# Running the mLSTM steps beside the attention, and preparing the first attention head earlier, in a two-layer hybrid trunk on one Trainium2 core

## The chip, the core and the metric

The kernel runs on one core of one Trainium2 (trn2) chip, as one launch. The metric is device time in microseconds (us). A profiled execution gives a trace of every engine: PE (TensorE: matrix products and transposes), DVE (VectorE), ACT (ScalarE), POOL (GpSimd), and SP, which here only issues DMAs. PE's clock has two levels, 1.2 and 2.4 GHz; the profile's "granted clock" is the mean over a stretch, 1.00 where all of it ran at 2.4 GHz and 0.50 where all of it ran at 1.2 GHz.

## What is computed

Two layers (L0 and L1) on 512 latent and 256 context tokens of width 1024. Each layer makes one input projection, feeds its columns to three token mixers, joins their outputs to a 1024-wide y, applies an output projection, and then a gated feed-forward network. In layer 1 the context rows are read but not written.

```
za, zb, zm = split(modulate(rmsnorm(x)) @ w_in)
ya = rwkv7_mixer(za)     # scan over tokens, then "post": norm, bonus, gate
yb = mla_mixer(zb)       # q = up(norm(cq)), k,v = up(norm(ckv)); softmax(q k^T / sqrt(96)) v, 8 heads
ym = mlstm_mixer(zm)     # chunkwise, two directions, 4 heads
x  = x + gate1 * (concat(ya, yb, ym) @ w_out)
x  = x + gate2 * swiglu(modulate(rmsnorm(x)))
```

## The kernel before

Tokens stand in six tiles of 128 (four latent, two context); the transposed activations of width 1024 are 128-row pages. Matrix products that need full precision are done as three products of split operands (high part times high part, high times low, low times high).

The program is written as one sequence of operations, and a scheduler then places each engine's instructions, in an order in which it expects them to become ready. So code that is written later can be placed earlier if its inputs and buffers are there. What a buffer's pool allows (how many buffers a name has, and when the pool opens) limits this. Once placed, each engine's order is fixed.

The parts of a layer that matter here, in order:

- The **RWKV scan** and the rest of the input projection, ending at about 416 us in L0 and 1640 us in L1.
- **mLSTM** (`mlstm`, from L1182): a preparation (six tiles of transposes), then `chunk` for i = 0..5 and both directions, 12 steps in all. A step takes PSUM tiles `pbc`, `pbg`, `pss`, `pn`, each a bank of its own (pool `pb`, one buffer a name). `finish` (L1293) normalises two token tiles after steps 3, 4 and 5. The sums are kept in a page `hs` of the page pool.
- **Up-projection** (`mla_up`, L840): `heads` computes k for all heads (L954), then q for heads 0 to 3 and 4 to 7 (L959), normalises and rotates them, transposes them per head (`by_channel`, L904) and stores them to DRAM (`ktd`, `qtd`). Then V (L968). It is written behind the mLSTM, and the scheduler places the two together.
- **Attention** (`mla_attend`, L972). `load(h)` (L982) reads k and q of a head into a raw tile `kq` (two buffers) and splits each into a high and a low tile. `maxima` (L1000) takes each query block's row maximum over the keys (PE L1008 into one 1024-wide PSUM tile `mx`, DVE L1010), transposes it (L1014) and writes it as row 96 of q's high tile (ACT L1015), so that the score product subtracts it. `attend` (L1018) makes, for each of the six key tiles, the scores (PE L1028 to L1030, tile `st`, two buffers), the exponentials (ACT L1032) and the value product (PE L1034) into `po` (two buffers). Column 64 of V is one, which yields the sum: it is copied (ACT L1039), transposed (L1042), inverted (L1044), spread (L1047) and multiplied in (L1050). In L0 a second, smaller range handles the context queries. Head h+1 is loaded, and its maxima taken, while head h attends. The pools of `mla_attend` open when those of `mla_up` have closed, so head 0's load stands behind the up-projection.
- **RWKV post** (`rwkv_post`, L725): one call of its generator after each of the heads 0 to 6 (`POSTA`), the rest behind the last head.
- The loads of X for the residual (L1329, L1331) and the output projection (L262).

Of the kernel before, what the change touches and what calls it, by code (L numbers as in the profile page):

```python
# [26 lines left out]
POST = (0, 0, 0, 0, 0)  # L27
POSTA = (1, 1, 1, 1, 1, 1, 1, 0)
YS = 0
FI = 3  # L30
MP = ((0, .4), (-1, 0))
# [145 lines left out]
def trunk(ctx, tc, I, out, dbg=None):  # L177
# [547 lines left out]
    def rwkv_post(l, ctx_out, data, y, wk, psum):  # L725
# [34 lines left out]
        for n in range(nn):  # L760
# [8 lines left out]
            py, pgt = psum[0](), psum[0]()  # L769
            for i in range(2):  # L770
                pe.transpose(py[:, i * P:(i + 1) * P], yt[:, 2 * n + i], ident)
                pe.transpose(py[:, 256 + i * P:256 + (i + 1) * P], bt[:, i * P:(i + 1) * P], ident)
                pe.matmul(pgt[:, i * P:(i + 1) * P], g2[:, i * P:(i + 1) * P], gd[:, n * P:(n + 1) * P],
                          start=True, stop=True)
# [5 lines left out]
            ve.tensor_tensor(t, t, py[:, 256:512], ALU.add)  # L780
            ve.scalar_tensor_tensor(y[:, 0:2, n * P:(n + 1) * P], t[:, :].rearrange("p (j t) -> p j t", j=2), 0.5,
# [58 lines left out]
    def mla_up(l, ctx_out, lat, wk, pm, krt, post, marks):  # L840

        steps = iter(POST)

        def fill():
            for _ in range(next(steps, 0)):
                next(post, None)
# [6 lines left out]
        units = 0  # L853

        def up(act, wt, n, M):

            nonlocal units
            ps = pm.tile([P, 512], F32, name="up")[:, :M]
            i = int(MP[l][0] + units * MP[l][1])
            units += 1  # L860
            for k in range(len(act)):
              with behind(marks[i:i + 1] if i >= 0 else ()):
                mm3(ps, [x[:, n * P:(n + 1) * P] for x in act[k]], wt[k], k == 0, k == len(act) - 1)
# [35 lines left out]
        def by_channel(src, H, dst, n, h0):  # L899

            for a in range(0, H, 4):
# [3 lines left out]
                t = wk.tile([96, 4, P], F32, name="stg", bufs=3)  # L905
# [3 lines left out]
        def heads(act, r, wt, n0, n1, H, w, extra, dst, h0):  # L909
# [5 lines left out]
            for n in range(n0, n1):  # L915
# [3 lines left out]
                sq = wk.tile([P, 512], F32, name="ksq")[:, :H * w].rearrange("p (h b) -> p h b", b=w)  # L919
# [25 lines left out]
        sq = wk.tile([P, 512], F32, name="ksq")[:, :NT * 32].rearrange("p (n c) -> p n c", c=32)  # L945
# [6 lines left out]
        fill()  # L952
        for n in range(0, NT, 2):
            heads(ckv, rkv, wt, n, n + 2, 8, 64, (kr2[:, :, 0], ks), ktd, 0)  # L954
            fill()
        for a in range(2):
# [3 lines left out]
            fill()  # L960
# [9 lines left out]
        return V  # L970

    def mla_attend(l, ctx_out, y, V, wk, wk2, pm, pv, post):  # L972
        nq = T if ctx_out else TL
        psum = lambda: pm.tile([P, 512], F32, name="mx")
# [5 lines left out]
        ac.activation(idr, ident, AF.Copy)  # L980

        def load(h):  # L982

            r = []
            for src, i, n in ((ktd, 1, T), (qtd, 0, nq)):
                t = wk.tile([96, T], F32, name="kq", bufs=2)[:, :n]
                dma = sp.dma_start(out=t, in_=src[h, :, :n])
                hi, lo = (w.tile([97, T], F32R, name=f"k{i}{j}", bufs=2)[:, :n] for j, w in enumerate((wk, wk2)))
                if i == 0:
                    ac.activation(hi[0:96], t, AF.Copy, scale=gain)  # L990
                    ve.scalar_tensor_tensor(lo[0:96], t, gain, hi[0:96].bitcast(F32), ALU.mult, ALU.subtract)
                else:
                    ac.activation(hi[0:96], t, AF.Copy)
                    gp.tensor_tensor(lo[0:96], t, hi[0:96].bitcast(F32), ALU.subtract)
                    gp.memset(hi[96:97].bitcast(F32), 1.0)
                r += [hi, lo]
            loads.append(dma)
            return r

        def maxima(kq, q0, q1, k0):  # L1000
            kh, kl, qh, ql = kq
            w = q1 - q0
            mr = wk.tile([P, 4], F32R, name="mr")
            for n in range(q0, q1):
                ps = pm.tile([P, 1024], F32, name="mx", bufs=1)
                for a, b in ((0, 512), (512, T)):
                    if a >= k0:
                        pe.matmul(ps[:, a - k0:b - k0], qh[0:96, n * P:(n + 1) * P], kh[0:96, a:b],  # L1008
                                  start=True, stop=True)
                ve.tensor_reduce(mr[:, n - q0:n - q0 + 1], ps[:, :T - k0], AX.X, ALU.max)  # L1010
                yield
            pt = pm.tile([P, 512], F32, name="pt")
# [3 lines left out]
            yield  # L1016

        def attend(h, kq, q0, q1, k0):  # L1018
# [6 lines left out]
            for kt in kts:  # L1025
# [5 lines left out]
                e = wk2.tile([P, 512], F32, name="pe", bufs=EB)[:, :w]  # L1031
# [6 lines left out]
            row = wk2.tile([P, 512], F32, name="row")[o:o + 1, :w]  # L1038
            ac.activation(row, po[o:o + 1, :w], AF.Copy)  # L1039
            pd = pm.tile([P, 512], F32, name="pt")  # L1040
            for n in range(q1 - q0):
                pe.transpose(pd[:, n:n + 1], row[:, n * P:(n + 1) * P], one128[o:o + 1, 0:1])  # L1042
            r = wk.tile([P, 4], F32, name="rden")
            ve.reciprocal(r[:, :q1 - q0], pd[:, :q1 - q0])  # L1044
            bc = pm.tile([P, 512], F32, name="pt")
            for n in range(q1 - q0):
                pe.transpose(bc[:, n * P:(n + 1) * P], r[:, n:n + 1].to_broadcast([P, P]), ident)  # L1047
            yo = y[hr, 2 + h // 2, qs]
            i = ac.activation(yo, po[hr, :w], AF.Copy)
            done.append((i, ve.tensor_tensor(yo, yo, bc[hr, :w], ALU.mult)))  # L1050

        ranges = ((0, 4, 0), (4, 6, 512))[:2 if ctx_out else 1]
        loads, done = [], []
        kq = load(0)
        for _ in maxima(kq, *ranges[0]):
            pass
        for h in range(8):
            ahead = [maxima(kq, *g) for g in ranges[1:]]
            if h < 7:
                kq2 = load(h + 1)  # L1060
# [469 lines left out]
```

## Time and profile before

| | us |
|---|---|
| median of 3 runs | 2279.31 (2273.39 to 2284.45) |
| the profiled execution, its own time | 2283.55 |
| its span in the trace | 2281.8 |
| PE busy | 2159.2 (95%), mean granted clock 0.959 |
| DVE, ACT, POOL busy | 1381.9 (61%), 844.7 (37%), 314.2 (14%) |
| chain that ended last, by engine | PE 81%, DVE 10%, ACT 4%, DMA 2%, issue 2% |

Read it in two steps. First the whole: PE is near full everywhere on average, so a change can only save where PE stands still or runs at the lower clock. Then the stage: the busy share of a stretch, its granted clock, and the chain of waits through it tell who held PE up.

### The profile page before, as it was taken

How to read it: one execution, taken by the hardware profiler on the slowest of the kernel's cores; microseconds unless marked ns; L12 is line 12 of the kernel's file. 1: busy time of each engine (PE TensorE's matmuls, PEld its weight loads, DVE VectorE, ACT ScalarE, POOL GpSimd, SP SyncE). 2: the span in 40 equal slices, each digit the busy share in tenths (PEclk: the TensorE clock that was granted, in tenths of full speed). 3: DMA queues.
4: the chain of work that ended last, by engine and by line, in shares of the span. 5: the costliest groups of instructions: out<-in, count | busy, mean ns of one | idle time of the engine just before them, and what ended most of it. 6: DMA issues, size and time to landing. Idle time of an engine off the chain costs nothing.

```text
span 2281.8 us, 36365 instructions
## 1 busy us (share of the span) xinstructions
PE 2159.2 (95%) x14604; PEld 1780.9 (78%) x14604; DVE 1381.9 (61%) x2706; ACT 844.7 (37%) x1527; POOL 314.2 (14%) x482
## 2 busy tenths in 40 slices
PE   7999997997999999999999999999898998999999
PEld 4788886784668788888888878787685677888887
DVE  6687777895547766554444455788796545334343
ACT  4433333664552421122122354433473544222231
POOL 1022322332201100000000111113142211000000
PEclk9999997897999999999999989999697998999999
DMA  7241112232115334344432312211232122323323
GB/s 289 84 153 52 62 41 74 77 88 56 42 70 155 100 114 146 111 129 135 133 112 83 109 52 63 73 57 39 85 100 59 35 74 83 101 94 94 100 92 102
DMA packets 87352, 211.99 MB, mean 93 GB/s; under 512 B 10248, under 2 KB 33680, under 8 KB 86544
## 3 DMA queue, kind: packets, MB, share of 16 engines
q1 hardware_dynamic: 87184, 209.67, 29.2%
q8 instruction: 115, 1.88, 0.3%
q14 instruction: 53, 0.43, 0.1%
HBM read 187.62 MB, written 22.02 MB: 92 GB/s over the span
## 4 chain that ended last, share of the span: by engine, by line
PE 81%; DVE 10%; ACT 4%; DMA 2%; issue 2%; POOL 1%; SPq 0%; DVEq 0%; ACTq 0%; POOLq 0%
PE gm L262 57%; PE po L1034 4%; PE psm L585 2%; PE inv L660 2%; PE st L1028 1%; DVE cT L320 1%; PE st L1029 1%; PE st L1030 1%; PE mx L1008 1%; PE psm L514 1%; PE pB L700 1%; DVE wl L228 1%; PE psm L573 1%; ACT hu L365 1%; PE up L246 1%
## 5 line engine op out<-in xcount | busy, mean ns | idle before, releaser
L262 PE MATMUL gm<-hpage,wh 128*128 128x512 f32 (+1 forms) x3744 | 1001.7, 355 | 15.3 <-ACT hpage L227 8.9
L262 PEld LDWEIGHTS gm<-hpage,wh 128*128 128x128 f32 x3744 | 664.2, 191 | 119.8 <-ACT hpage L227 11.0
L262 PE MATMUL gm<-hpage,wl 128*128 128x512 f32 (+1 forms) x1872 | 657.4, 353 | 1.9 <-DVE wl L228 1.8
L227 ACT ACTIVATE wh<-wr 128x1024 fp32r<-128x1024 f32 (+2 forms) x214 | 221.6, 1036 | 560.7 <-PE gm L262 457.6
L262 PEld LDWEIGHTS gm<-hpage,wl 128*128 128x128 f32 x1872 | 358.1, 191 | 50.6 <-DVE wl L228 2.5
L228 DVE TENSOR_TENSOR wl<-wr,wh 128x1024 fp32r<-128x1024 f32 (+2 forms) x214 | 258.2, 1207 | 186.9 <-ACT wh L227 185.1
L262 PE MATMUL gm<-hid,wh 128*128 128x512 f32 (+1 forms) x1056 | 282.6, 356 | 0.0
L262 PEld LDWEIGHTS gm<-hid,wh 128*128 128x128 f32 x1056 | 185.6, 188 | 32.2
L262 PE MATMUL gm<-hid,wl 128*128 128x512 f32 (+1 forms) x528 | 187.4, 356 | 0.0
L1323 DVE SCALAR_TENSOR_TENSOR X<-gm,mod,X 128x512 f32<-128x512 f32 (+1 forms) x100 | 64.0, 643 | 191.0 <-PE gm L262 187.7
L320 DVE CUSTOM_DVE_ANT_0 cT<-wd,cB,mod_b 128x1024 f32<-128x1024 f32 x140 | 177.7, 1300 | 1.1 <-DMA wd<-in_mod_d 0.7
L1492 DVE SCALAR_TENSOR_TENSOR ft<-ft,gm 128x512 f32<-128x512 f32 x66 | 39.5, 598 | 153.0 <-PE gm L262 152.7
L1010 DVE TENSOR_REDUCE mr<-mx 128x1 fp32r<-128x768 f32 (+1 forms) x80 | 67.9, 848 | 83.8 <-PE mx L1008 83.6
L1034 PE MATMUL po<-pe,hpage 128*128 128x512 f32 (+1 forms) x224 | 112.2, 590 | 0.5 <-ACT pe L1032 0.4
L262 PEld LDWEIGHTS gm<-hid,wl 128*128 128x128 f32 x528 | 99.0, 188 | 16.1
L338 POOL TENSOR_TENSOR acc<-acc,sq 128x512 f32<-128x512 f32 (+1 forms) x15 | 23.9, 1601 | 604.0 <-ACT sq L337 604.0
L1032 ACT ACTIVATE pe<-st 128x512 f32<-128x512 f32 (+1 forms) x112 | 62.9, 563 | 89.8 <-PE st L1030 88.7
L227 ACT ACTIVATE hid<-ft 128x512 fp32r<-128x512 f32 x66 | 36.2, 549 | 128.4 <-DVE ft L1492 128.4
L1028 PE MATMUL st<-k,k 97*128 97x512 f32 (+1 forms) x112 | 78.0, 698 | 4.7 <-ACT k L1015 4.1
L1490 ACT ACTIVATE ft<-gm 128x512 f32<-128x512 f32 x66 | 33.9, 514 | 90.4 <-PE gm L262 90.3
L1008 PE MATMUL mx<-k,k 96*128 96x256 f32 (+1 forms) x144 | 46.3, 396 | 17.1 <-DVE mr L1010 9.9
L585 PE MATMUL psm<-pr,kb 64*128 64x128 f32 (+1 forms) x384 | 57.7, 308 | 1.4 <-POOL pr L555 1.4
(425 smaller groups left out, 3128.5 us busy)
## 6 DMA issues: line engine op xcount, KB each, us to landing
wr<-in_ffn_in SPq DMA_DIRECT2D x88, 512.0 KB, 3.5
wd<-in_mod_d SPq DMA_DIRECT2D x86, 512.0 KB, 3.8
wr<-in_w_in SPq DMA_DIRECT2D x44, 512.0 KB, 3.6
wr<-in_ffn_out SPq DMA_DIRECT2D x34, 448.0 KB, 3.4
wr<-in_w_out SPq DMA_DIRECT2D x20, 512.0 KB, 3.7
wr<-in_ffn_out SPq DMA_DIRECT2D x16, 512.0 KB, 3.6
zs<-ze SPq DMA_DIRECT2D x26, 256.0 KB, 2.0
X<-in_xT SPq DMA_DIRECT2D x16, 384.0 KB, 6.4
```

The costliest lines, as they stand in the source:

```text
L227: ac.activation(hi, src, AF.Copy)
L228: return en.tensor_tensor(lo, src, hi.bitcast(F32), ALU.subtract)
L262: pe.matmul(ps, x[:, j], act[k][y][:, a:b], start=(i == 0 and n == 0), stop=(i == len(kl) - 1 and n == 2))
L320: ve.tensor_tensor_reduce(out=t[:, s], in0=w, in1=cb[:, s], scale=1.0, scalar=modb[:, l, m:m + 1], op0=ALU.mult, op1=ALU.add, accum_out=mo ...
L585: pe.matmul(pa[j][:, p, c], flat(kb[hr, d, p, c]), flat(pr[hr, d, p, c, 0:nq]), start=True, stop=True)
L660: i = pe.matmul(v8(o)[hr, q], a[hr, d, p, c], b[hr, d, p, c], start=True, stop=True)
L1008: pe.matmul(ps[:, a - k0:b - k0], qh[0:96, n * P:(n + 1) * P], kh[0:96, a:b], start=True, stop=True)
L1010: ve.tensor_reduce(mr[:, n - q0:n - q0 + 1], ps[:, :T - k0], AX.X, ALU.max)
L1028: pe.matmul(ps, kh[0:97, ks], qh[0:97, qs], start=True, stop=False)
L1032: ac.activation(e, ps, AF.Exp, scale=QK_SCALE)
L1034: pe.matmul(po[:, :w], v, e, start=(kt == kts[0]), stop=(kt == kts[-1]))
L1323: return ve.scalar_tensor_tensor(X[:, m, a:b], ps, mods[l][:, 24 * which + 16 + m, s:s + 1], X[:, m, a:b], ALU.mult, ALU.add)
```

## The change

- The mLSTM becomes a generator. Its preparation runs first; then `mla_up` takes one step after every second call of `heads` (`SIDE[l][2]` = 2), and `mla_attend` takes the rest between key tiles, in proportion to the key tiles done. RWKV post is taken in the same way: two mLSTM steps, then one of post (`turns`). `POST`, `POSTA` and `MP` (which made some products wait for mLSTM marks) go.
- `between()`, behind the first half of the q projection, loads head 0 and takes its maxima. For this `mla_heads` has pools of its own (`q`, `px`).
- PSUM: all mLSTM and post tiles share the name `m` with two buffers (before, four names with a bank each). The maxima take two 512-wide tiles (two buffers) with one reduction each, and a maximum of the two. `po` and `pt` go from two buffers to one.
- `load` has no raw tile. k goes straight into a page of the page pool (the low half first holds the raw k). q goes into `qs`, one buffer in each of two pools, the low half holding the raw q. The gain is applied to q, the POOL subtraction to k, as before.
- After a head, one ACT copy of the whole of `po` to `ov` replaces the two copies L1039 and L1049, and y is written by the final multiplication.
- `hs` is kept in y itself instead of a page.

```diff
-POST = (0, 0, 0, 0, 0)
-POSTA = (1, 1, 1, 1, 1, 1, 1, 0)
+SIDE = (0, 60, 2), (0, 46, 2)
...
 # mla_up
         for n in range(0, NT, 2):
             heads(ckv, rkv, wt, n, n + 2, 8, 64, (kr2[:, :, 0], ks), ktd, 0)
-            fill()
+            step()
...
+            if a == 0:
+                between()
...
+        def load(h, wk):
+
+            k = hp.tile([P, 2, T], F32R, name="hpage")
+            q = wk.tile([97, 2, T], F32R, name="qs", bufs=1)
+            kh, kl, qh, ql = k[0:97, 0], k[0:97, 1], q[:, 0, :nq], q[:, 1, :nq]
+            raw = lambda t: t[0:96].bitcast(F32)
+            sp.dma_start(out=raw(kl), in_=ktd[h])
+            ac.activation(kh[0:96], raw(kl), AF.Copy)
+            gp.tensor_tensor(kl[0:96], raw(kl), raw(kh), ALU.subtract)
+            gp.memset(kh[96:97].bitcast(F32), 1.0)
+            loads.append(sp.dma_start(out=raw(ql), in_=qtd[h, :, :nq]))
+            ac.activation(qh[0:96], raw(ql), AF.Copy, scale=gain)
+            ve.scalar_tensor_tensor(ql[0:96], raw(ql), gain, raw(qh), ALU.mult, ALU.subtract)
...
 # maxima
-                ps = pm.tile([P, 1024], F32, name="mx", bufs=1)
...
-                ve.tensor_reduce(mr[:, n - q0:n - q0 + 1], ps[:, :T - k0], AX.X, ALU.max)
+                for i, (a, b) in enumerate(rng):
+                    ps = px.tile([P, 512], F32, name="mx")[:, :b - a]
+                    pe.matmul(ps, qh[0:96, n * P:(n + 1) * P], kh[0:96, a:b], start=True, stop=True)
+                    o = m2[:, i] if len(rng) == 2 else mr
+                    ve.tensor_reduce(o[:, n - q0:n - q0 + 1], ps, AX.X, ALU.max)
...
 # attend
-            po = pv.tile([P, 512], F32, name="po")
+            po = pv.tile([P, 512], F32, name="po", bufs=1)
...
-            ac.activation(row, po[o:o + 1, :w], AF.Copy)
+            ov = wk.tile([P, 512], F32, name="ov", bufs=2)[:, :w]
+            i = ac.activation(ov, po[:, :w], AF.Copy)
...
                 for _ in attend(h, kq, *g):
                     next(ahead, None)
                     next(ahead, None)
+                    at += 1
+                    while got < SN and (at - first) * (SN - got0) > (got - got0) * (over - first):
+                        next(side, None)
+                        got += 1
...
 # mlstm: chunk
-            pbc = pm.tile([P, 512], F32, name="pbc")
+            pbc = pm.tile([P, 512], F32, name="m")
...
-        hs = hp.tile([P, NT, 256], F32, name="hpage")
+        hs = [y[:, 6:8, n * P:(n + 1) * P] for n in range(NT)]
...
+        psb = lstack.enter_context(pool(f"pb{l}", 2, space=PSUM))
+        px = lstack.enter_context(pool(f"px{l}", 2, space=PSUM))
+        qp = lstack.enter_context(pool(f"q{l}", 1))
...
+            def between():
+                kq.append(heads[0](0, qp))
+                for _ in heads[1](kq[0], *RANGES[0], lambda: pm.tile([P, 512], F32, name="bc")):
+                    pass
```

How the placed order changes, at three places. (Line numbers are those of the program before or of the changed one, which are a few apart: maxima L1008 and L1005, scores L1028 and L1035, value products L1034 and L1041.)

PE in layer 0, the end of the up-projection, before (`up` and `bc` are the up-projection's tiles, `pss` mLSTM's, `mx` the maxima):

```order
L248 MATMUL up<-wh,hpage 128x512
L904 MATMUL bc<-c_id,kn 96x128 x8
L1307 MATMUL pss<-c_id,hpage 128x128 x6
L1008 MATMUL mx<-k_5829,k_5836 128x512
L1008 MATMUL mx<-k_5829,k_5836 128x256
```

PE in layer 0, head 0's maxima in the changed program (`m` is an mLSTM tile):

```order
L246 MATMUL up<-wh,hpage 128x384
L1271 MATMUL m<-mva,m_5616 128x65 x4
L1246 MATMUL m<-c_id,Q 128x128 x4
L1005 MATMUL mx<-hpage,qs 128x512
L1005 MATMUL mx<-hpage,qs 128x256
```

and the beginning of its attention, where the first scores follow the up-projection directly:

```order
L246 MATMUL up<-wh,hpage 128x512
L1237 MATMUL m<-c_id,sb 128x128
L901 MATMUL bc<-c_id,kn 96x128 x4
L1246 MATMUL m<-c_id,Q 128x128 x4
L901 MATMUL bc<-c_id,kn 96x128 x4
L1268 MATMUL m<-C_4685,qd 128x260
L1292 MATMUL m<-mva,kd_6137 128x260
L1237 MATMUL m<-c_id,sb 128x128
L1035 MATMUL st<-qs,hpage 128x512
```

The maxima moved from behind the last piece of the up-projection to a place some 67 rows ahead of the first scores, with the V projection between. Eight of the twelve mLSTM steps of layer 0 still stand ahead of the first scores; four, and two of three `finish`, now stand among the scores of heads 0 to 2.

ACT in layer 1, around the end of a head in the middle, before (`kq` the raw tile, `row` and `y` the copies of a finished head, `pt` the maxima's transpose):

```order
L1032 ACTIVATE pe<-st 128x512
L993 ACTIVATE k_17438<-kq 96x768
L1032 ACTIVATE pe<-st 128x512
L990 ACTIVATE k_17445<-kq,qkgain 96x512
L1039 ACTIVATE row<-po 1x512
L1015 ACTIVATE k_17334<-pt 1x512
L1049 ACTIVATE y<-po 64x512
L1032 ACTIVATE pe<-st 128x512 x4
```

and in the changed program:

```order
L1039 ACTIVATE pe<-st 128x512 x6
L225 ACTIVATE hpage<-y 128x512
L1014 ACTIVATE qs<-pt 1x512
L992 ACTIVATE qs<-qs,qkgain 96x512
L1046 ACTIVATE ov<-po 128x512
L1039 ACTIVATE pe<-st 128x512 x6
```

The conversion of the next-but-one head's q stood behind an exponential and converted an older raw tile; it now converts a tile that its own DMA fills, and the copy `ov` and the next head's exponentials stand behind it.

SP in layer 0, the last head loads and X, before:

```order
L987 DMA kq<-ktd 96x768
L987 DMA kq<-qtd 96x768
L1329 DMA X<-in_xT 128x768 x8
L318 DMA wd<-in_mod_d 128x1024 x4
```

and in the changed program:

```order
L991 DMA qs<-qtd 96x768
L987 DMA hpage<-ktd 96x768
L1335 DMA X<-in_xT 128x768 x8
L316 DMA wd<-in_mod_d 128x1024 x3
L991 DMA qs<-qtd 96x768 x3
L316 DMA wd<-in_mod_d 128x1024
```

X and three weight loads moved ahead of the q loads of heads 5, 6 and 7.

## Rows read from the trace of the kernel before

**Rows 1.** The page: busy time, share of the span, instructions of each engine
```profile
PE 2159.2 (95%) x14604; PEld 1780.9 (78%) x14604; DVE 1381.9 (61%) x2706; ACT 844.7 (37%) x1527; POOL 314.2 (14%) x482
```
**Rows 2.** Windows: stretch, length, busy PE, PEld, DVE, ACT, POOL, clock, DMA, GB/s
```profile
416.70:511.20 94.50, 88.36 (x543) 77.43 (x541) 89.27 (x304) 61.82 (x137) 35.91 (x54) 1.00 0.26 73
511.20:533.90 22.70, 6.24 (x18) 3.99 (x18) 11.58 (x23) 5.62 (x9) 3.98 (x3) 0.59 0.43 118
533.90:557.00 23.10, 21.71 (x80) 15.21 (x81) 9.90 (x20) 10.96 (x21) 2.55 (x2) 0.81 0.09 27
557.00:668.40 111.40, 105.74 (x489) 73.23 (x488) 57.62 (x113) 62.05 (x122) 22.49 (x17) 1.00 0.08 22
668.40:673.20 4.80, 3.78 (x28) 3.02 (x29) 1.46 (x5) 3.00 (x7) 0.00 (x0) 1.00 0.00 0
1650.00:1721.90 71.90, 68.59 (x433) 59.21 (x429) 63.26 (x206) 49.38 (x108) 28.44 (x44) 0.99 0.30 87
1721.90:1738.40 16.50, 9.81 (x33) 6.61 (x31) 11.46 (x42) 2.77 (x5) 4.00 (x4) 0.56 0.31 86
1738.40:1770.00 31.60, 29.60 (x85) 18.21 (x86) 16.56 (x33) 13.44 (x25) 6.62 (x6) 0.75 0.16 47
```
**Rows 3.** Chain that ended last, 511 to 535 us: start, us, what
```profile
514.04 6.21 DMA kq<-ktd
522.03 1.80 DVE k L991
523.85 3.23 DMA kq<-qtd
531.60 0.97 DVE mr L1010
```
**Rows 4.** The same chain, 1719 to 1740 us
```profile
1723.18 4.23 DMA kq<-ktd
1734.12 0.97 DVE mr L1010
```
**Rows 5.** The same chain, 664 to 690 us
```profile
672.36 0.35 SPq L1329
676.41 8.90 DMA wd<-in_mod_d
```
**Rows 6.** PE waits, 416 to 534 us: total, times, longest
```profile
PE pn L1263 <- DVE qd L1238: 2.9, 3, 1.5
PE pbc L1286 <- DVE qd L1238: 0.5, 1, 0.5
```
**Rows 7.** Tile kq, layer 1, its last line
```profile
DMA to landing us min/median/max: 3.0/3.1/4.2
```
**Rows 8.** ACT groups, 385 to 1860 us: count, busy, mean ns, idle before
```profile
L1032 ACT ACTIVATE pe<-st 128x512 f32<-128x512 f32 x96 | 56.9, 594 | 84.8 <-PE st L1030 83.8
L1258 ACT ACTIVATE m<-pbg,Q 128x128 f32<-128x128 f32 x80 | 22.8, 373 | 18.9 <-PE pn L1266 9.7 <-PE pbg L1241 9.1
L1039 ACT ACTIVATE row<-po 1x512 f32<-1x512 f32 x16 | 9.4, 588 | 12.1 <-PE po L1034 12.1
L990 ACT ACTIVATE k<-kq,qkgain 96x512 fp32r<-96x512 f32 x8 | 5.7, 710 | 0.0
L1039 ACT ACTIVATE row<-po 1x256 f32<-1x256 f32 x8 | 3.0, 375 | 1.3 <-PE po L1034 1.2
```
**Rows 9.** DVE groups, 385 to 1860 us
```profile
L1010 DVE TENSOR_REDUCE mr<-mx 128x1 fp32r<-128x768 f32 x64 | 61.1, 955 | 73.7 <-PE mx L1008 73.5
L1253 DVE TENSOR_TENSOR m<-pss,c_tri 128x512 f32<-128x512 f32 x10 | 6.8, 683 | 0.1
L1010 DVE TENSOR_REDUCE mr<-mx 128x1 fp32r<-128x256 f32 x16 | 6.8, 423 | 10.1 <-PE mx L1008 10.0
```
**Rows 10.** PE timeline, layer 1's last heads: start, us, operation, [idle before]
```profile
1827.93 0.41 PE L1042 MATMUL pt<-one,row 1*128 1x1 f32 x4 [0.22 <-ACT row L1039]
1828.64 0.47 PE L1028 MATMUL st<-k,k 97*128 97x512 f32 x1 [0.30 <-ACT k L1015]
1829.88 0.40 PE L1030 MATMUL st<-k,k 96*128 96x512 f32 x1
1830.12 0.51 PE L1008 MATMUL mx<-k,k 96*128 96x512 f32 x2
1830.47 0.60 PE L1047 MATMUL pt<-c_id,rden 128*128 128x128 f32 x4
1850.55 2.04 PE L1034 MATMUL po<-pe,hpage 128*128 128x512 f32 x4
```

More of the change, by code (lines that the diff above doesn't have):

```diff
@@ L780, in rwkv_post @@
             ve.tensor_tensor(t, t, py[:, 256:512], ALU.add)
+            pgt = psum()
+            for i in range(2):
+                pe.matmul(pgt[:, i * P:(i + 1) * P], g2[:, i * P:(i + 1) * P], gd[:, n * P:(n + 1) * P],
+                          start=True, stop=True)
             ve.scalar_tensor_tensor(y[:, 0:2, n * P:(n + 1) * P], t[:, :].rearrange("p (j t) -> p j t", j=2), 0.5,
@@ L838, in latent, with mla_up, step @@
         return parts, rs
[L840 to L846, printed above, removed]
+    def mla_up(l, ctx_out, lat, wk, pm, krt, between, side):
+        at = got = 0
+        def step():
+            nonlocal at, got
+            at += 1
+            if at % SIDE[l][2] == 0:
+                next(side, None)
+                got += 1
         nq = T if ctx_out else TL
@@ L980, in mla_attend @@
         ac.activation(idr, ident, AF.Copy)
[L982 to L998, printed above, removed]
@@ L1000, in maxima @@
-        def maxima(kq, q0, q1, k0):
+        loads = []
+        def load(h, wk):
[10 more added lines that the diff above has]
+            ve.scalar_tensor_tensor(ql[0:96], raw(ql), gain, raw(qh), ALU.mult, ALU.subtract)
+            return kh, kl, qh, ql
@@ L1016, in maxima, with mla_attend @@
             yield
+        return load, maxima, loads
+    RANGES = ((0, 4, 0), (4, 6, 512))
+    SN = 22
+    def mla_attend(l, ctx_out, y, V, heads, kq, qp, wk, pm, pv, side, got):
+        load, maxima, loads = heads
+        psum = lambda: pm.tile([P, 512], F32, name="pt")
         def attend(h, kq, q0, q1, k0):
@@ L1037, in attend @@
             o = 64 - 32 * (h % 2)
[L1038 to L1040 removed]
+            ov = wk.tile([P, 512], F32, name="ov", bufs=2)[:, :w]
+            i = ac.activation(ov, po[:, :w], AF.Copy)
+            pd = psum()
             for n in range(q1 - q0):
[L1042 removed]
+                pe.transpose(pd[:, n:n + 1], ov[o:o + 1, n * P:(n + 1) * P], one128[o:o + 1, 0:1])
             r = wk.tile([P, 4], F32, name="rden")
             ve.reciprocal(r[:, :q1 - q0], pd[:, :q1 - q0])
[L1045 removed]
+            bc = psum()
             for n in range(q1 - q0):
                 pe.transpose(bc[:, n * P:(n + 1) * P], r[:, n:n + 1].to_broadcast([P, P]), ident)
[L1048 to L1056, printed above, removed]
+            done.append((i, ve.tensor_tensor(y[hr, 2 + h // 2, qs], ov[hr], bc[hr, :w], ALU.mult)))
+        ranges = RANGES[:2 if ctx_out else 1]
+        done, at = [], 0
+        first, over, _ = SIDE[l]
+        got0 = got
         for h in range(8):
[L1058 removed]
+            ahead = [maxima(kq, *g, psum) for g in ranges[1:]]
             if h < 7:
[L1060 to L1061 removed]
+                kq2 = load(h + 1, (qp, wk)[(h + 1) % 2])
+                ahead.append(maxima(kq2, *ranges[0], psum))
             ahead = chain(*ahead)
@@ L1066, in mla_attend @@
                     next(ahead, None)
+                    at += 1
+                    while got < SN and (at - first) * (SN - got0) > (got - got0) * (over - first):
+                        next(side, None)
+                        got += 1
             for _ in ahead:
                 pass
-            with behind(done[-1]):
-                for _ in range(POSTA[h]):
-                    next(post, None)
             kq = kq2
-        for _ in post:
+        for _ in side:
             pass
@@ L1342, in behind, with turns @@
         return st
+    def turns(a, b):
+        while True:
+            n = 0
+            for g in (a, a, b):
+                for _ in g:
+                    n += 1
+                    yield
+                    break
+            if n == 0:
+                return
     early = ExitStack()
```

96 lines of the change are left out of this document (43 added, 53 removed).

## The prediction, made before the changed kernel was run

> **What bounds the kernel now.** The page comes first: PE is busy 95% of the span [rows 1], so time can only be won where PE stands or runs slowly. Next come the windows around the two places that the change touches [rows 2]. The reader is to see four things there. In the up-projection stages PE is busy 88.36 of 94.50 us (layer 0) and 68.59 of 71.90 (layer 1), at full clock. Then there is a hole in each layer: 22.70 us with PE busy for 6.24 at a granted clock of 0.59, and 16.50 us with 9.81 busy at 0.56. Behind each hole stands a stretch at reduced clock: 23.10 us at 0.81, and 31.60 us at 0.75. The rest of the attention of layer 0 is full again, 105.74 of 111.40. The chain of waits says who made the holes. In layer 0 it goes through the load of head 0's k (6.21 us to landing), a DVE subtraction, the load of its q (3.23), and then maxima, one block after the other [rows 3]; in layer 1 through the same load (4.23) and the maxima [rows 4]. So the holes are head 0's preparation, which nothing covers, and the slow stretches are what they leave behind: the clock is low in the hole, and full again only well into the attention.
>
> **The change, part by part.**
>
> *Head 0 moved into the projection.* The placed order shows it: the maxima now stand far ahead of the first scores, and the first scores come right behind the last pieces of the up-projection. What the holes hold of PE's work stays. Scaled to full clock it is at most 6.24 x 0.59 = 3.7 us and 9.81 x 0.56 = 5.5 us. Free: 22.7 - 3.7 = 19.0 and 16.5 - 5.5 = 11.0, together **30.0 us**. The two loads that are moved stand in SP's queue among the stores and weight loads of the projection; their landing (3 to 6 us [rows 3, 4]) has the V projection and the second half of q to hide under.
>
> *The slow stretches.* A stretch of length t at clock c would take t x c at full clock, if PE fills it. That frees 23.10 x 0.19 = 4.4 us and 31.60 x 0.25 = 7.9 us [rows 2], 12.3 in all. I take **10**, since a new short wait may bring a bit of it back; bounds 0 (if another hole appears) and 12.3.
>
> *mLSTM and post steps moved into the attention.* PE's own work only changes its place: it leaves a stage that PE fills to 94% and goes into one filled to 95% [rows 2], so I cost the move itself at nothing. What covers DVE's part is slack there: DVE is busy 57.62 of 111.40 us in the attention against 89.27 of 94.50 in the projection. If the attention had no PE work to hide under, the moved DVE work would show. Since the projection's DVE is relieved, its 6.1 and 3.3 us of PE idle might go too: 0 to 9.4 us, and I take 0, because other work (post's first part) is drawn into the same stage.
>
> *The end of layer 0's attention.* The last post block stood behind the last head: 4.80 us with PE busy 3.78 [rows 2]. Its work moves, its idle time goes: **1 us**.
>
> *Two reductions for one.* A 768-wide reduction costs 0.955 us. Instead: one of 256 (0.423) and one of 512, for which the nearest row is another 512-wide read of PSUM, 0.683 [rows 9]. That is 0.15 us more for each of 64 blocks, 10 us of DVE over both layers, plus a tiny maximum. In the attention DVE has 54 us to spare in layer 0 alone, so: nothing. Head 0's part, in the busy projection stage, is paid for by the steps that left.
>
> *One buffer for `po` and `pt`.* At the end of a head (or range) the next value product must wait for the copy `ov`. It is one ACT copy, 0.588 us at 512 columns and 0.375 at 256 [rows 8]; there are 16 of the first and 8 of the second. Before that product stand the six score products of the next head, from 1828.64 to 1830.12, 1.5 us [rows 10], which need no `po`. So I cost it at nothing. The upper bound is every copy in full: 16 x 0.588 + 8 x 0.375 = 12.4 us. The Trainium skill (Perfetto Trace Analysis, Optimizing Tensor Performance) says that independent matmul groups should rotate through different PSUM banks so that the evacuation of one overlaps the matmuls of the next, which the single `po` gives up; by that rule the sum would be about 12 us worse, 2260. No row before shows it, since `po` had two.
>
> *Two banks instead of four for mLSTM.* Each step's tiles now wait for each other. In the projection of layer 0 PE waited 3.4 us for mLSTM results with four banks [rows 6]. I take the same once more over both layers, **4 us**. The lower bound is 0; the upper is one further wait of four activations (4 x 0.373 = 1.5 us [rows 8]) for each of the 20 steps with an output, 30 us.
>
> *q without a raw tile.* The largest unknown. q of head h+2 goes into the buffer that head h reads until its last score, so its DMA starts there. Call that moment T. It lands at T + 3.1 [rows 7] and is converted by T + 3.8 (0.71 [rows 8]). Behind the conversion, on ACT, stand `ov` (T + 4.4) and the first exponential (T + 5.0). PE has, behind T, two value products (2.04 us), six scores (1.5) and a pair of maxima (0.35) [rows 10]: 3.9 us. Then it waits 0.5 for `ov`, and after the sum's transposes (0.25) another 0.35 for the exponential: 0.85 us, where 0.52 is waited at this place today (0.22 and 0.30 [rows 10]). I take 0.5 us for heads 2 to 7 of both layers, **6 us**. Bounds: 0, and the whole 3.8, 46 us. The loads of X and three weights now precede the q of heads 5 to 7 in layer 0's queue. Today the first weight lands at 685.3, 13 us after the first X load is issued [rows 5]; X can go once post is done, in head 3, so it should be over before head 5's q is due. I add nothing.
>
> **The sum.** 30.0 + 10 + 1 - 4 - 6 = 31 us. The profiled execution took 2283.55, so 2252.5; it lies 4.2 above the median of the runs shown, 2279.31, and on that footing the forecast is **2248 us**. Between holes closed with no new wait at all (30.0 + 12.3 + 1 + 9.4 = 52.7) and the rivals below lies all that I expect.
>
> **Rivals.**
>
> *Everything closes.* The new waits are hidden, and the projection loses its idle time: 2279.3 - 52.7 = 2227. For it: every new wait found has a cover of nearly its size. Against: the attention keeps 5% idle even with its second buffers [rows 2].
>
> *The banks give it back.* Every `ov` is exposed (12.4) and a third of mLSTM's bound (10): 2248 + 22 = 2270. For it: mLSTM steps stand between scores on PE, in an order fixed beforehand, so a late tile stops the scores behind it. Against: only four steps of layer 0 stand there.
>
> *The hole moves to head 1.* The change then does not do what it says: head 1's q cannot be loaded before the projection's buffers are released and its last store is out, so PE would stand at head 1's maxima instead. Price: load and conversion (4.2 + 0.7 [rows 4, 8]), twice, and the slow stretch behind (12.3): 22 us, 2270. Against: the order puts four key tiles of scores, over 6 us of PE work, ahead of those maxima.
>
> *Slower: q holds ACT at every head.* The conversion stands ahead of the next head's exponentials. If it comes as late as 3.8 us beyond PE's own work, scores fill their two buffers and PE stops; after such a stop part of the next stretch runs at half clock, as behind the holes. With 2 us lost that way (4.4 and 7.9 were lost behind the far longer holes): 12 x (3.8 + 2.0) = 70 us instead of 6, 2248 + 64 = 2312. The change breaks even at (31 + 6) / 12 = 3.1 us a head, and is slower by over 0.5% from 4.0. Against: the 3.9 us of PE work behind T. The Trainium skill (TensorE: Matmul & The Clock Gate, Architectural detail) calls ACT's queue strict FIFO, so that no exponential could pass the waiting conversion; the rows here show no wait long enough to test it.
>
> **How the numbers follow.** Chances: forecast 0.56 (2237 to 2260), everything closes 0.14, banks 0.17, hole moves 0.05, slower 0.08. The range leaves out the slower case and the tails of the two at 2270: **2226 to 2272**. A measurement of this kernel can tell about 0.5%, 11.4 us, from no change. Below 2267.9 lie the first two and almost half of the banks' case: 0.78. Within 0.5%: the rest of it and the moved hole, 0.14. Slower: 0.08.
>
> **What will show it.** If right, in the changed profile no stretch of 10 us between the projection and the attention has PE under 80% busy, and the granted clock there stays near 1.00 in both layers. Waits of scores, value products and sums on ACT stay under 1 us a head. DVE's share in the attention rises above 60%. It is wrong if a wait of PE on the q conversion, or on `ov`, repeats at each head with more than 2 us, if the time per head in layer 0 grows after its mLSTM steps are done, or if a hole stands at head 1.

## The result, and the profile after

| | before | changed |
|---|---|---|
| median, us | 2281.88 (4 runs, 2273.39 to 2290.82) | 2308.84 (4 runs, 2306.99 to 2311.31) |
| ratio | | 1.0118, 95% interval 1.0077 to 1.016 |
| span of the profiled execution, us | 2281.8 | 2305.9 |
| mean granted clock | 0.959 | 0.962 |

The change made the kernel slower by 1.2%; 1.4% faster had been forecast. The first row of the changed kernel's page answers to [rows 1]: PE is busy 11.6 us longer, and idle for 135.1 us instead of 122.6.

```profile
PE 2170.8 (94%) x14604; PEld 1783.4 (77%) x14604; DVE 1388.2 (60%) x2786; ACT 832.2 (36%) x1503; POOL 312.4 (14%) x482
```

The windows answer to [rows 2]. The columns are the same; the stretches are, in each layer, from the first to the last piece of the up-projection, from there to the first scores, and then two parts of the attention. Between the same events, the first two stretches of each layer before were:

```profile
422.10:509.90 87.80, 81.87 (x500) 72.29 (x500) 83.05 (x290) 57.79 (x127) 32.73 (x49) 1.00 0.28 79
509.90:533.90 24.00, 7.33 (x28) 4.84 (x26) 12.56 (x27) 6.88 (x10) 4.35 (x3) 0.62 0.41 112
1654.80:1718.90 64.10, 61.31 (x365) 53.40 (x364) 58.06 (x190) 45.19 (x98) 26.24 (x39) 1.00 0.33 95
1718.90:1738.40 19.50, 12.29 (x51) 8.79 (x49) 14.19 (x51) 5.60 (x11) 5.02 (x6) 0.62 0.26 73
```

and in the changed kernel:

```profile
421.80:523.30 101.50, 86.14 (x467) 70.48 (x466) 84.28 (x280) 55.48 (x116) 37.96 (x48) 0.95 0.29 77
523.30:527.90 4.60, 2.63 (x20) 1.84 (x17) 2.18 (x5) 4.56 (x10) 1.72 (x5) 1.00 0.77 191
527.90:551.00 23.10, 19.60 (x94) 13.88 (x94) 18.31 (x44) 12.69 (x26) 7.66 (x8) 1.00 0.22 67
551.00:683.10 132.10, 125.15 (x557) 88.39 (x558) 62.73 (x152) 63.88 (x124) 13.18 (x14) 0.92 0.16 54
1663.90:1739.10 75.20, 64.25 (x327) 51.60 (x325) 62.61 (x199) 42.32 (x86) 29.73 (x40) 0.93 0.33 89
1739.10:1752.10 13.00, 10.11 (x61) 8.47 (x60) 10.68 (x28) 7.45 (x14) 7.98 (x8) 0.87 0.34 99
1752.10:1783.70 31.60, 27.34 (x106) 18.84 (x105) 18.22 (x49) 14.99 (x31) 7.05 (x8) 0.84 0.18 51
1783.70:1876.50 92.80, 87.86 (x340) 56.63 (x338) 42.91 (x98) 40.65 (x71) 6.97 (x7) 0.94 0.12 40
```

In layer 0 the hole is closed: 4.60 us where 24.0 lay between the last piece and the first scores. But the projection, which PE filled to 93%, is now filled to 85% (86.14 of 101.50), and its last piece ends at 523.3 instead of 509.9. So the first scores of layer 0 start only 6 us earlier (527.90 against 533.86), and the attention then takes 155 us instead of 134. Part of that is work that moved there (PE is busy for 144.8 us instead of 127.5), part the clock (0.93 over the whole of it instead of 0.97). The time did not vanish with the hole; it moved to both sides of it.

In layer 1 the hole is not closed: 13.0 us remain of 19.5, better filled. Three of the four pairs of head 0's maxima still stand behind the last piece, which ends at 1739.1 (PE's timeline):

```profile
1736.15 0.62 PE L1005 MATMUL mx<-hpage,qs 96*128 96x512 f32 x2 [1.07 <-ACT qs L992]
1740.35 0.59 PE L1005 MATMUL mx<-hpage,qs 96*128 96x512 f32 x2
1742.09 0.71 PE L1005 MATMUL mx<-hpage,qs 96*128 96x512 f32 x2 [0.71 <-DVE m L1007]
1744.55 0.72 PE L1005 MATMUL mx<-hpage,qs 96*128 96x512 f32 x2
```

The projection there is 11 us longer as well (75.2 against 64.1).

Who holds PE inside the projection? Three of the largest waits of PE there (layer 0, 421 to 528 us: total, times, longest), all on other engines' results:

```profile
PE mx L1005 <- DVE m L1007: 5.1, 2, 3.1
PE bc L901 <- DVE kn L933: 4.4, 3, 3.3
PE m L1292 <- ACT m L1263: 1.8, 2, 1.4
```

The first is head 0's own maxima. The chain of waits through the second (start, us, what) shows a new guest: `yt` L761 is the end of RWKV post's first part (its statistics and norm), which the old program held behind head 0 and which now stands on DVE in front of the k norm (`kn` L933). The same wait of PE stands in e9 below (4.5 us), which leaves post free, and in neither e1 nor e4, which hold it.

```profile
435.84 2.02 DVE yt L761 x2
437.86 1.03 DVE kn L933
439.02 1.93 PE bc L901 x8
```

### The profile page after: what moved, and what is told of

Its sections match the earlier page's. It is cut to its first block, busy times and chain, and to the rows that moved or that the text cites. A ratio compares the mean times of both kernels' runs of the same rounds, so it can differ in the third digit from the quotient of the medians.

```text
span 2305.9 us, 36379 instructions
## 1 busy us (share of the span) xinstructions
PE 2170.8 (94%) x14604; PEld 1783.4 (77%) x14604; DVE 1388.2 (60%) x2786; ACT 832.2 (36%) x1503; POOL 312.4 (14%) x482
## 4 chain that ended last, share of the span: by engine, by line
PE 81%; DVE 9%; ACT 4%; DMA 3%; issue 1%; POOL 0%; SPq 0%; ACTq 0%; DVEq 0%; POOLq 0%
PE gm L260 58%; PE po L1041 4%; PE psm L583 2%; PE inv L658 2%; PE st L1035 1%; PE st L1036 1%; PE st L1037 1%; PE psm L512 1%; DMA qs<-qtd 1%; DMA lz<-zs 1%; PE pB L698 1%; PE mx L1005 1%; DVE hu L362 1%; PE psm L571 1%; DVE wl L226 1%
## 5 line engine op out<-in xcount | busy, mean ns | idle before, releaser
L1041 PE MATMUL po<-pe,hpage 128*128 128x512 f32 (+1 forms) x224 | 112.2, 594 | 1.1 <-ACT pe L1039 0.8
L1007 DVE TENSOR_REDUCE m<-mx 128x1 f32<-128x512 f32 (+1 forms) x128 | 66.0, 551 | 56.7 <-PE mx L1005 56.3
L1039 ACT ACTIVATE pe<-st 128x512 f32<-128x512 f32 (+1 forms) x112 | 62.3, 565 | 100.5 <-PE st L1037 99.7
L1035 PE MATMUL st<-qs,hpage 97*128 97x512 f32 (+1 forms) x112 | 76.7, 685 | 2.0 <-ACT stg L903 1.5
L1005 PE MATMUL mx<-hpage,qs 96*128 96x256 f32 (+1 forms) x144 | 50.7, 424 | 11.9 <-DVE m L1007 8.4
```

The costliest lines, as they stand in the source:

```text
L1005: pe.matmul(ps, qh[0:96, n * P:(n + 1) * P], kh[0:96, a:b], start=True, stop=True)
L1007: ve.tensor_reduce(o[:, n - q0:n - q0 + 1], ps, AX.X, ALU.max)
L1035: pe.matmul(ps, kh[0:97, ks], qh[0:97, qs], start=True, stop=False)
L1039: ac.activation(e, ps, AF.Exp, scale=QK_SCALE)
L1041: pe.matmul(po[:, :w], v, e, start=(kt == kts[0]), stop=(kt == kts[-1]))
```

## The experiments

All are given as the median and the ratio to the kernel before on the same chip. **First round**: undo one suspect each, then all three. e1 takes a step of post only when a head is done, and behind it:

```diff
 # turns(side, post)
+                if g is b and not done:
+                    continue
+                with behind(done[-1] if g is b else ()):
```

> Post of the RWKV mixer is taken only once head 0 has finished, as in the kernel before. Theory 'DVE in the projection': the 12 us a layer of post's statistics on DVE, which now stand inside the up-projection, hold up the k and q norms there; taking them out removes most of the extra idle time of that stage (19 us in layer 0 against 6 before, 21 us in layer 1 against 3): 2285 to 2298 us. Rival 'two banks': the up-projection lost time because mLSTM's tiles share two banks; then this run stays within 4 us of 2309 and PE still waits there on mLSTM tiles.

Measured: **2277.72**, 0.9982 (0.9967 to 0.9996): 31 us less than the change, more than its theory had. The windows of e1 (first piece to first scores but for the last 0.8 us; attention) show the projection 5 us shorter than the change's 101.5, with no hole behind it, and an attention as long as the change's 155.2. The projection also starts 4 us earlier. In the change part of the statistics stands in the end of the scan, but that this is the reason isn't shown: with post held, e11's projection starts at 425.4. In layer 1 the projection takes 62.6 us instead of 75.2.

```profile
417.30:513.40 96.10, 86.16 (x471) 72.24 (x470) 80.98 (x256) 54.19 (x111) 37.59 (x47) 0.93 0.30 83
514.20:669.00 154.80, 144.34 (x660) 102.70 (x661) 93.53 (x243) 82.30 (x164) 24.99 (x26) 0.94 0.18 60
```

e2 moves X:

```diff
-            with behind(loads[3:4]):
+            with behind(loads[7:8]):
                 xload(X, l)
```

> Only the loads of X wait, behind the q load of head 7 instead of head 3. Theory 'X in front of q': q of head 5 landed 8 us after its issue at 612 us because 3 MB of X and 1.5 MB of weights were ahead of it, its maxima came bunched behind head 4, and that head's slot took 22.7 us instead of 16.5; without X ahead of it the run gets 4 to 7 us faster, 2302 to 2305. Rival: the maxima of head 5 were late because of q's single buffer and would have been late anyway; then within 2 us of 2309.

Measured: **2299.69**, 1.0076 (1.0049 to 1.0103), 9 us less, again more than its theory had. SP's timeline of the change (start, us, operation) shows what e2 took away, and the loads of q tell it too (landing, minimum/median/maximum: 2.8/3.5/8.2 in the change, 2.8/3.1/3.9 in e2):

```profile
603.44 4.30 SPq L1335 DMA_DIRECT2D X<-in_xT  x8
607.78 2.83 SPq L316 DMA_DIRECT2D wd<-in_mod_d  x3
612.12 15.42 SPq L991 DMA_DIRECT2D qs<-qtd  x2
```

e3 gives q a third buffer:

```diff
-                kq2 = load(h + 1, (qp, wk)[(h + 1) % 2])
+                kq2 = load(h + 1, *((wk, 2) if (h + 1) % 3 else (qp,)))
```

> q has three buffers instead of two, so the load of head h+2 no longer waits for head h's last score. Theory 'q load exposed': PE's waits at the first maxima on the q conversion (1.25 us at head 4 of layer 0, 0.8 in layer 1) and the half-clock stretches behind them (some 2 us each) go: 6 to 14 us, 2295 to 2303. Rival: the end of each head is held by the single banks of po and pt, whatever q does; then within 3 us of 2309.

Measured: **2288.66**, 1.0022 (1.0005 to 1.0039), 20 us less, more than either case had. e4 has all three edits:

> All three edits together. If the three causes are separate and together hold most of what the closed holes won, the gains add: 2309 minus 20 to 35, that is 2274 to 2289, about the kernel before. If the two-bank rival holds, it stays above 2295.

Measured: **2268.97**, 0.994 (0.9919 to 0.9961), below its range. 40 us, not the sum of 60: the causes overlap.

**Second round**, on e4: what are the change's own parts worth? e5 puts head 0's preparation back behind the projection (`i` is the copy of its last piece):

```diff
-            if a == 0:
-                between()
...
+        with behind((i,)):
+            between()
         return V, got
```

> The kernel with all three edits (2269), but head 0's load and maxima stand behind the last piece of the up-projection, as before the change; everything else stays. Theory 'the hole was worth what the prediction said': 30 us of idle time and some 10 of low clock come back, less a few us that head 0's maxima cost inside the projection: 2294 to 2309. Rival: mLSTM steps, which may now stand in the hole, cover much of it; then 2272 to 2285.

Measured: **2264.77**, 0.9915 (0.9885 to 0.9944): head 0 late again, and no slower; it lies below both ranges. The windows of layer 0 of e4 (projection, attention) and then of e5 (projection, place of the hole, attention) show why:

```profile
420.20:518.70 98.50, 86.38 (x471) 72.58 (x470) 80.95 (x257) 54.01 (x111) 38.38 (x47) 0.93 0.29 81
519.50:664.80 145.30, 138.09 (x660) 97.80 (x661) 89.27 (x243) 81.24 (x164) 26.12 (x26) 0.99 0.20 64
```
```profile
419.40:499.00 79.60, 72.35 (x422) 62.03 (x421) 69.49 (x227) 49.70 (x102) 34.95 (x43) 1.00 0.35 98
499.00:517.00 18.00, 13.01 (x57) 8.65 (x54) 16.27 (x35) 9.15 (x15) 9.23 (x8) 0.77 0.39 117
517.00:658.60 141.60, 138.24 (x659) 98.99 (x658) 86.24 (x240) 77.45 (x159) 21.97 (x23) 0.97 0.16 53
```

First piece to first scores takes 99.3 us with head 0 early and 97.6 with it late. The projection alone is 19 us longer with it early, and PE's idle time on the whole way is the same: 12.1 us in e4's projection, 7.3 and 5.0 in e5's two stretches. In the place of the hole DVE is now busy 16.27 of 18.00 us, and PE 13.01 (in the kernel before, between the same two events, 12.56 and 7.33 of 24.0): mLSTM steps stand in it, which in the old program's layer 0 were all ahead of it. This pair tests layer 0 only: in layer 1, e4's first scores come 18.3 us behind the last piece and e5's 16.4, since there head 0's maxima stand behind the last piece in e4 too (three of four pairs, as in the change).

e6 and e7 move one bank from the maxima (two tiles to one) to mLSTM's tiles, and to `pt`:

```diff
-        px = lstack.enter_context(pool(f"px{l}", 2, space=PSUM))
+        px = lstack.enter_context(pool(f"px{l}", 1, space=PSUM))
```

> All three edits, and mLSTM's tiles get three banks; the maxima give one up and have one. Theory 'two banks': the waits of PE in front of mLSTM products in the projection (some 10 us in layer 0, 5 in layer 1 in the run with all three edits) are in good part turns of the two banks: 2258 to 2266. Rival 'DVE in the projection': those products wait for DVE's work whatever the banks, and the single tile of the maxima costs some: 2268 to 2280.

> All three edits, and the small tile at a head's end (transposed maxima, sums, reciprocals) gets a second bank; the maxima give one up. Theory 'single pt': the waits of 0.3 to 1.5 us at the ends of heads are its turns: 3 to 8 us, 2261 to 2266. Rival: the single tile of the maxima costs as much or more: 2268 to 2280.

Measured: **2362.97** (1.0345, 1.0317 to 1.0373) and **2339.19** (1.0245, 1.0221 to 1.027). They say nothing of the banks that were given, since the bank taken away cost 94 and 70 us against e4. The waits of PE in e6 (layer 0, 400 to 690 us) are led by

```profile
PE mx L1005 <- DVE m L1007: 15.0, 17, 2.5
```

(in e4 the same line has 0.6, once).

e8 holds all mLSTM steps that are written into the attention behind its first exponential.

> All three edits, and the mLSTM steps that are written into the attention may not be placed ahead of its first exponential: four stay in each projection, eight go into the attention. Theory 'DVE in the projection is the bound': moving their DVE work out shortens the projection by 10 us or more a layer, and the attention, with DVE under 60% busy, takes the PE work at its price: 4 to 12 us faster, 2257 to 2265. Rival 'moved work brings its waits': in the attention's order each step's chain PE, DVE, ACT, PE holds the scores behind it, and the time stays or grows: 2268 to 2285.

Measured: **2289.78**, 1.0037 (1.0016 to 1.0059): about 21 us slower than e4, the rival's way and beyond its range. Projection and attention of its layer 0:

```profile
420.30:510.40 90.10, 76.47 (x402) 64.16 (x400) 63.62 (x201) 47.38 (x89) 32.95 (x38) 0.91 0.31 87
511.20:673.00 161.80, 152.90 (x726) 109.49 (x727) 108.82 (x297) 87.98 (x186) 29.17 (x35) 0.95 0.18 58
```

The projection loses 8 us against e4 and the attention gains 16.5: here moved work was not free.

**Third round.** e9 is the change with only e5's edit, e10 the kernel before with only post's first part set free (`behind` dropped for head 0). e11 is e5 with four banks for mLSTM during the projection (the maxima's two open behind it), and e12 is e11 with head 0's loads free to go early.

> The change as it is (2309), with one thing undone: head 0's load and maxima stand behind the last piece of the up-projection again. Theory 'the hole was DVE's, not PE's': head 0's maxima cost the DVE-bound projection what they save behind it, so the time stays: 2300 to 2312. Rival, the prediction's step: holes and cold stretches are worth 30 to 40 us, so this run is slower than the change: 2335 to 2350.

> The kernel before, with one thing of the change: the first part of RWKV post (its statistics) is no longer held behind head 0 and may be placed as early as its inputs allow. Theory 'post's 12 us of DVE in the projection': 10 to 30 us slower than before, 2292 to 2312. Rival 'only together with the two banks and head 0's maxima': within 5 us of before, 2277 to 2287.

> The run with head 0 behind the projection (2265), and mLSTM's tiles get four banks while the projection runs (the maxima's two banks are not open then). In the placed order all mLSTM steps then stand inside the projection and none is left for the hole or the attention. Theory 'mLSTM as cover': the hole stands open again and 8 to 20 us come back: 2273 to 2285. Rival 'two banks': the projection wins more than that from free banks: 2250 to 2262.

> As the run before, but only the maxima of head 0 stand behind the projection; its loads and conversions may go as early as the data are there. Theory 'the hole is load first, maxima second': the 6 and 3 us of the two loads and the conversions (about 10 us a layer in the chain of the kernel before) are hidden, 8 to 20 us less than the run before: 2255 to 2270. Rival 'DVE': the same DVE work has to be done before the first scores wherever the loads stand; within 4 us of the run before.

Measured: e9 **2277.97**, 0.9979 (0.9958 to 0.9999); e10 **2288.62**, 1.003 (1.0014 to 1.0046), between its two cases; e11 **2261.18**, 0.9906 (0.9884 to 0.9928), and e12 **2258.05**, 0.9886 (0.9861 to 0.9912), the fastest version here. e11's time is the rival's, but by another way: in its place of the hole PE is busy for only 6.76 of 17.4 us, so the cover is gone as the theory has it; the first scores come 2 us later than in e5 (99.7 us behind the first piece), and the attention, rid of mLSTM, is 2 us shorter (139.7). The place of the hole is 17.4 us long even so, against 24.0 before. Two loads stood in the chain of waits through it before (6.21 and 3.23 us [rows 3]); in e5's and e11's there is none. e12's 3 us less than e11 are no more than the spread, as its rival said. e5, e11 and e12 can't be told apart for certain.

e9 is the surprise, outside both of its cases: undoing the early head 0 alone wins 31 us. Its windows (projection, place of the hole, attention) show that they are not in the hole:

```profile
423.00:508.40 85.40, 76.61 (x417) 65.12 (x416) 72.71 (x246) 52.06 (x108) 34.51 (x44) 0.93 0.34 90
508.40:526.20 17.80, 13.24 (x58) 9.72 (x56) 14.83 (x30) 8.81 (x15) 9.20 (x8) 0.73 0.37 107
526.20:664.80 138.60, 136.81 (x665) 98.26 (x664) 78.92 (x202) 76.84 (x152) 17.89 (x21) 0.99 0.17 56
```

To the first scores it takes 103.2 us against the change's 106.1. It is the attention that is 16.6 us shorter, with 1.8 us idle and a clock of 0.99. Layer 1 has 10 us more: 67.8 us instead of 75.2 in its projection, and 120.1 instead of 124.4 from the first scores to the last value product.

**Fourth round**: are e1's and e9's 31 us the same ones (e13: both edits)? Is head 1's q late (e14: e9 with that load held behind head 0's row maxima)? Is the attention's loss q and X (e15: e2's and e3's edits together; e16: these and e5's)?

> The change with both things undone at once: post held behind head 0, and head 0's load and maxima behind the projection (q keeps two buffers). Each alone gave 2278, 31 less than the change. Theory 'one bound, DVE in the projection, overloaded by either': once one of them is out, the other costs little, so the second brings 4 to 14 us more: 2264 to 2274. Rival 'two separate costs': they add, 2309 minus 62: 2240 to 2252.

> The change with head 0 behind the projection (2278), but q of head 1 is loaded only once head 0's row maxima are written, as late as it is in the change itself, where its buffer opens with the end of the projection. Theory 'head 1 becomes the late one': part of what the early head 0 costs is that nothing then covers head 1's load and maxima; 5 to 12 us slower than 2278, in layer 0's heads 0 and 1: 2283 to 2290. Rival: head 1 has slack; within 3 us of 2278.

> The change with the third q buffer and with X behind the last q load; post free and head 0 early, as in the change. Theory 'the attention's loss is q': in the profile of the change the attention of layer 0 loses 20 us to idle time and low clock at the ends of heads, 16 more than with head 0 late, and layer 1's as much; with q early enough both go and the run is as fast as with head 0 late: 2274 to 2284. Rival: q's buffer gave 20 us and X has nothing left to give, the rest is the maxima's own lateness: 2285 to 2290.

> As the run before, with head 0's load and maxima behind the projection again. If closing the hole wins nothing by itself once q is out of the way, within 5 us of the run before. If the early head 0 costs something of its own (its maxima in the DVE-bound projection), 8 us or more faster than it; if it wins something, slower.

Measured: e13 **2277.94**, 0.9982 (0.9965 to 0.9999), e14 **2279.22**, 0.9977 (0.9959 to 0.9996), e15 **2285.5**, 1.0021 (1.0005 to 1.0037), e16 **2282.07**, 1.0006 (0.9992 to 1.002). Head 1 has slack (e14), e15 stops at the edge of its rival's case, and e16 is within 5 us of it, its first case. e13 fits neither of its cases: the second edit brings nothing at all. Together the runs make two squares, in us:

| | head 0 early | head 0 late |
|---|---|---|
| q two buffers, X early: post free | 2309 (the change) | 2278 (e9) |
| same, post held | 2278 (e1) | 2278 (e13) |
| q three buffers, X late: post free | 2285 (e15) | 2282 (e16) |
| same, post held | 2269 (e4) | 2265 (e5) |

With q and X out of the way the lower square adds up: post free costs 17 us in either column, and the early head 0 is worth nothing in either row (3 to 4 us worse, inside the spread of the runs). Post's price can be found in layer 1's projection: from first to last piece it takes 61.6, 62.0 and 64.5 us in e4, e5 and e13, which hold post, and 68.5, 68.0, 67.8 and 75.2 in e15, e16, e9 and the change; it takes 64.1 in the kernel before, and 73.4 in e10. Read as a ladder from the kernel before (2281): everything undone 2265, the early head 0 +4, post free +17, q's two buffers and the early X +23. That is one order of several. The upper square doesn't add: post free and the early head 0 cost 31 us together, and neither costs anything without the other; q and X cost 23 us in one cell, 9 and 13 in two, and nothing in e9's.

**Where q's load is paid.** The difference lies in PE's order. In the change, head 4's first maxima (594.12) stand ahead of head 3's scores; head 2's last score, which frees q's buffer, is at 589.29. PE's timeline of the change:

```profile
589.29 0.28 PE L1037 MATMUL st<-qs,hpage 96*128 96x256 f32 x1
592.26 0.61 PE L779 MATMUL m<-wa,g 128*128 128x128 f32 x4
594.12 0.62 PE L1005 MATMUL mx<-hpage,qs 96*128 96x512 f32 x2 [1.25 <-ACT qs L992]
595.00 0.40 PE L1049 MATMUL pt<-one,ov 1*128 1x1 f32 x4 [0.26 <-ACT qs L1014]
595.34 0.50 PE L1035 MATMUL st<-qs,hpage 97*128 97x512 f32 x1
```

and of e9, at the same place, where six scores and a step of post stand in between and nothing waits:

```profile
580.59 0.28 PE L1037 MATMUL st<-qs,hpage 96*128 96x256 f32 x1
583.72 0.50 PE L1035 MATMUL st<-qs,hpage 97*128 97x512 f32 x1
585.66 0.61 PE L779 MATMUL m<-wa,g 128*128 128x128 f32 x4
586.03 0.48 PE L1005 MATMUL mx<-hpage,qs 96*128 96x512 f32 x1
```

Two heads on it is DVE's queue. The chain of waits of the change, 627 to 634 us (head 6's q is loaded, head 5's row maxima and scores wait):

```profile
627.22 2.93 DMA qs<-qtd
630.23 0.94 ACT qs L992
631.20 1.01 DVE qs L993
632.43 0.65 PE pt L1013 x4
633.10 0.60 ACT qs L1014
```

and DVE's timeline there: the merging of head 5's maxima (L1010), which has had its inputs since the reduction at 629.44 was over, stands behind head 6's q.

```profile
629.44 1.02 DVE L1007 TENSOR_REDUCE m<-mx 128x1 f32<-128x512 f32 x2
631.20 1.01 DVE L993 SCALAR_TENSOR_TENSOR qs<-qs,qkgain 96x768 fp32r<-96x768 f32 x1 [0.74 <-ACT qs L992]
632.13 0.15 DVE L1010 TENSOR_TENSOR mr<-m 128x4 fp32r<-128x4 f32 x1
```

The windows around it: 2.9 us idle in 8.2, and then 5.8 us at half clock, which cost as much again.

```profile
626.00:634.20 8.20, 5.33 (x29) 3.88 (x27) 6.41 (x13) 3.98 (x7) 0.00 (x0) 0.95 0.13 36
634.20:640.00 5.80, 5.80 (x17) 4.29 (x16) 2.05 (x5) 1.19 (x2) 0.00 (x0) 0.50 0.01 3
```

## Why the prediction was wrong

- **"Head 0 moved into the projection", 30 us: the step that failed first.** It took the holes' idle time as free once the work was placed elsewhere, and looked for cover on PE alone. In layer 0 the stage that received the work had DVE busy for 89.27 of 94.50 us [rows 2], as nearly full as PE, and head 0's reductions are DVE's: the hole closed, the projection grew by 14 us (87.8 to 101.5), and PE waits 5.1 us in it on those reductions. That DVE's load is the whole reason is argued from these shares and waits. In layer 1 the work was not moved: the placed order had been read for layer 0, and in layer 1 three of four pairs of maxima stand behind the last piece. So of the 11.0 us there little could come: 13.0 us lie between last piece and first scores, and 14.2 in e9, which puts head 0 back. For the whole kernel the move cost 31 us in the change (e9) and was worth nothing once q and X were out of the way (e4 against e5, e15 against e16). What does shorten the way to layer 0's first scores in e5, from 111.8 to 97.6 us, is not the early head 0; mLSTM steps in the hole are worth some 2 us of it, judged by e11, which has more banks too, and the rest was not taken apart.
- **"The slow stretches", 10 us.** The clock came back right behind the hole (1.00 in 527.9 to 551), and was lost again at later stops: 0.92 over the rest of layer 0's attention, 0.84 and 0.94 in layer 1's. The projections lost clock too: 0.95 and 0.93, where they had 1.00. The prediction had allowed for "a new short wait"; there were several.
- **"mLSTM and post steps moved", at nothing.** Two errors. Post's first part, of which the prediction said that it is drawn into the projection, was set against the relief of DVE there instead of being priced: 17 us with q and X out of the way (e4 to e15, e5 to e16), 31 in the change itself (e1), 7 on the kernel before (e10). And mLSTM steps forced into the attention cost some 21 us (e8), though DVE has slack there. DVE's share of layer 0's attention, which was to rise above 60%, is 52% (81.03 of 155.2 us).
- **"q without a raw tile", 6 us, and X at nothing.** Together 23 us (e15 to the change). The sum put six scores between the freed buffer and the first maxima; the scheduler had placed them behind. That the conversion can hold a queue was one rival's mechanism, and it was DVE's queue that was seen held, not ACT's. That rival's 2312 lies near 2309, but it is not what happened: it had 70 us for q alone, at every head, and both holes closed, which layer 1's is not. X was said to be over before head 5's q is due: it could only start when post was done, at 603.4, and that q took 8.2 us.
- **Right:** a 512-wide and a 256-wide reduction for the 768-wide one (0.15 us more expected; 0.688 + 0.414 against 0.955, by the groups below); `po` with one buffer at nothing (in the whole attention of layer 0 the value products waited 0.3 us for `ov`, and the transposes that read it 1.8 in three waits), against an upper bound of 12. Two banks for mLSTM at 4 us is not refuted, but not shown either: four in e11 took 4 us less than e5, within the spread, and the placed order changed with them.

```profile
L1007 DVE TENSOR_REDUCE m<-mx 128x1 f32<-128x512 f32 x64 | 44.0, 688 | 51.0 <-PE mx L1005 50.7
L1007 DVE TENSOR_REDUCE m<-mx 128x1 f32<-128x256 f32 x64 | 26.5, 414 | 5.7 <-PE mx L1005 5.6
```

**Open:** why head 0's maxima come so late in layer 1; why the scheduler, with head 0 early, puts a head's first maxima ahead of the scores before it, and with head 0 late behind them; and so why the upper square doesn't add; and which of the parts that were left in place makes e5 16 us faster than the kernel before. Two banks for `po` weren't tried: none of the eight is free.

## What to carry to other kernels

Before work is moved out of a hole in one engine, see that the stage that takes it has room on the engine that the work itself uses: read that engine's share there, not only the stalled one's. Then read the placed order in every layer: the same code can be placed early in one and late in another. When a program is rewritten so that old ordering constraints fall away, list what else becomes free to move, and price each piece in the stage to which it can go. Where a buffer is freed late, count the cover behind it from the placed order, and look at every in-order queue that the refill passes, not only the busiest.

## What the runs showed of the hardware that was not expected

- One PSUM bank less for a product that DVE reduces at once cost 94 and 70 us of e4's 2269 (4.1% in e6, 3.1% in e7), net of what the bank was worth where it went, and far more than every other bank question here. The Trainium skill (Perfetto Trace Analysis, Optimizing Tensor Performance) asks for such groups to rotate through banks; here it holds for the maxima, and had next to no price for `po` (0.3 us of waits of the value products in layer 0's attention).
- A 288 KB load of q that takes 3.1 us by itself took 8.2 behind 3 MB of X and 1.5 MB of weights on the same queue.
- Stops of 1.5 and 2.9 us were followed by stretches at granted clocks of 0.66 (595 to 600 us) and 0.50 (634.2 to 640).
